# A list scheduler's model of DMA, a rule on PSUM banks, and a new table of tie offsets

## The chip, the cores and the metric

The kernel runs on one core of one Trainium2 chip. The metric is the device time of one execution in microseconds (us), lower is better. The time before is the median of three runs.

## What is computed

One layer of a streaming encoder for a prompt of 1024 frames and a sample of 32 frames with 512 frames of past, model width 1024. Half of the mixer is band attention (8 heads of 64, called A), half is stick-breaking attention (8 heads of 64, called B). All of it is in float32.

```python
u = rmsnorm(h, g_pre) @ w_in                     # q k v gate of A, q k v gate of B
# A: each frame reads its own 64-frame chunk and the 8 chunks before it
s = einsum(q, k) * scale + bias_table[:, rel];   w = softmax(where(ok, s, -1e30))
# B: strictly causal
z = einsum(q, k) * scale
log_beta = log_sigmoid(z);  log_1m = where(causal, log_sigmoid(-z), 0)
after = cumsum(log_1m, reverse) - log_1m
w = where(causal, exp(log_beta + after), 0)
o = einsum(w, v)
# end of the layer
y = concat([oa * silu(ga), ob * silu(gb)]) @ w_out
h = h + rmsnorm(y, g_post)
h = h + sigmoid(h @ w_ple_gate) * (p @ w_ple)
```

The new keys and values of both groups are outputs too.

## The kernel before

The 1056 rows (1024 of the prompt and 32 of the sample) are worked on as three chunks of 352. Every product in float32 is made of three products of rounded parts: high by high, high input by low weight, low input by high weight. Names with an h at the end (wTh, wh_kA, hnh) are high parts, with an l (wTl, wl_kA, hnl) low parts.

The work is cut into stages. The stage "first" loads x, normalises it, turns it on TensorE (ptx), makes the product of p with w_ple (ple) and the first projections (mm_kA, mm_qA, mm_vA). Stages 0 to 7 are the eight pairs of heads A0 B0 A1 B1 A2 B2 A3 B3; in each, the attention of the pair's two heads is woven with the projections of the next pair, and in the last stages with the gate projections (mm_gA, mm_gB; a chunk is 24 matmuls). The sample's heads come in between (names with an s: sA0, sB1). The stage "last" makes the output product and the gate product of the end, each cut Strassen-like into sets of seven products (o0P to o3P, then g0P to g3P).

A tile of attention is 128 queries against up to 1024 keys. Its name has the pair, the head and the tile: B31_4 is tile 4 of the second head of pair B3. TensorE makes the scores into a bank of PSUM called S, as a product with the keys' high part (kd) and one with their low part (kl). ScalarE, VectorE and GpSimd make the weights of them. The weights must then be turned. For most tiles TensorE does that (ptw). For tiles 5, 6, 7 of A and 4, 5, 6 of B, VectorE turns blocks of 32 x 32, one DMA writes the tile to a scratch in DRAM (swap), four DMAs read it back as the low tile wTl, ScalarE casts the high part out of it (wTh), and GpSimd or VectorE subtracts. Then sets of matmuls multiply with the values (PVA, PVB); a set takes several tiles. For keys, GpSimd makes the low part klB on one half of the partitions, and a DMA copies it to the other half (klB<-klB). Gate chunks go from PSUM through ScalarE (sg, three buffers in turn; sggA, sggB in the trace) and GpSimd, where they are multiplied with the attention's output (oggA, oggB, read back from the scratch o_dr), to the scratch og_dr, and from there as uo, lo, whole left inputs, into the output product. PSUM's eight banks are shared out as mm 2, S 3, T 2, PV 1; in the stage "last" the product sets and ple take turns at them too. The weights of the output product come as woB (the block whose two sums and casts give oB) and woT.

All DMAs go over one queue that SP fills. The order on every engine is set as follows. A recorder takes down every operation without issuing it (class Recorder). Then order(), line 478, runs a list scheduler: each engine has a heap of operations whose inputs are there at the engine's free time, and takes the one with the smallest key. The key is a class and the number at which it was recorded, plus an offset in AHEAD_OF by engine, first letters of the written tile's name, and stage. cost() gives each operation a duration. A DMA is modelled as an issue of 550 ns, 1500 ns more to its start (DMA_NS), one line for all transfers at 320 bytes a nanosecond, and 2000 ns to its completion (DMA_MARGIN). emit() (line 548) issues in this order; its line 558 is the line of all instructions in the trace. In the built program each engine runs its instructions in that order and waits on semaphores. A DMA also waits, on SP, for one of eight semaphores of the transfers eight places ahead.

Of the kernel before, what the change touches and what calls it, by code (L numbers as in the profile page):

```python
# [10 lines left out]
AF = mybir.ActivationFunctionType  # L11
# [15 lines left out]
NT = 9  # L27
STAGES = ("first", 0, 1, 2, 3, 4, 5, 6, 7, "last")
AHEAD_OF = {
# [4 lines left out]
    ("ACT", "hnh"): (26, 0, 0, 0, 0, 0, 0, 0, 0, 0),  # L34
# [4 lines left out]
    ("ACT", "pleo"): (-50, 0, 0, 0, 0, 0, 0, 0, 0, 0),  # L39
    ("ACT", "sg"): (0, 0, 0, 0, 0, 0, 0, 0, 0, 67),  # L40
    ("ACT", "stk"): (0, 0, 0, 0, -177, -400, 75, 0, 0, 0),
    ("ACT", "stq"): (0, 122, -152, -75, 154, 366, 0, 0, 0, 0),
    ("ACT", "stv"): (0, 0, 19, 0, 0, -79, 0, 25, 0, 0),
    ("ACT", "vt"): (234, 0, 0, 0, 0, 0, 0, 0, 0, 0),
    ("ACT", "wTh"): (0, 12, -62, 30, 74, -241, 0, 102, 0, 0),
    ("ACT", "wh"): (0, 0, 236, -23, 0, 0, 0, 0, 203, -9),
    ("ACT", "whS"): (0, 0, 0, 0, 0, 0, 0, 0, 0, 37),
    ("ACT", "x"): (0, 0, 0, 0, 0, 0, 0, 0, 0, -7),
    ("ACT", "yb"): (0, 0, 0, 0, 0, 0, 0, 0, 0, 427),
    ("DVE", "Kcs"): (0, 0, 0, 0, 402, 0, 0, 0, 102, 0),  # L50
# [5 lines left out]
    ("DVE", "diags"): (0, 0, 0, 400, 0, 0, 0, 0, 0, 0),  # L56
# [4 lines left out]
    ("DVE", "ogg"): (0, 0, 0, 0, 0, 0, 0, 0, 200, 0),  # L61
    ("DVE", "om"): (0, -187, -50, -41, -135, 385, -331, 253, -174, 0),
    ("DVE", "rb"): (265, 0, 0, 0, 0, 0, 0, 0, 0, 0),
    ("DVE", "sgg"): (0, 0, 0, 0, 0, 0, 0, 0, -180, 0),
# [4 lines left out]
    ("DVE", "wTl"): (0, -75, 64, 0, -385, 0, 0, 0, 0, 0),  # L69
# [8 lines left out]
    ("POOL", "ksS"): (0, 0, 0, 0, 0, 0, 0, 70, 0, 0),  # L78
    ("POOL", "om"): (0, 0, -289, 0, 0, 0, -89, 0, 0, 0),
    ("POOL", "ug"): (0, 0, 0, 0, 0, 0, 0, 0, 0, -100),  # L80
    ("POOL", "wTl"): (0, 493, 327, 0, 0, 0, 0, 0, 0, 0),
# [24 lines left out]
}  # L106


# [152 lines left out]


class Op:
    __slots__ = ("eng", "what", "args", "kw", "key", "busy", "late", "ready", "left", "after", "at", "size", "shared", "table", "kind")


LAND = {"PE": 165, "ACT": 0, "DVE": 0, "POOL": 0, "SP": 0, "CTL": 0}
SEM = 60
MARGIN = 400
ISSUE = 550  # L270
TABLE = 1280
DMA_NS, DMA_RATE, DMA_MARGIN = 1500, 320.0, 2000
DVE_SET, POOL_SET = 137, 110


# [78 lines left out]
class Recorder:  # L354
# [37 lines left out]
    def node(self, eng, what, args, kw, after):  # L392
        o = Op()
        o.eng, o.what, o.args, o.kw, o.after = eng, what, args, kw, after
        o.key = (self.cls if eng == "PE" else self.low, len(self.ops), len(self.ops))
        o.shared, o.table, o.kind = False, None, None
        self.ops.append(o)
        return o

    def add(self, eng, what, args, kw):  # L400
        writes, reads = [], []
# [7 lines left out]
        o = self.node(eng, what, args, kw, set())  # L409
# [20 lines left out]
        if writes:  # L430
            name = str(writes[0].buf.name)
            kind = (eng, name[:next((i for i, x in enumerate(name) if x.isdigit() or x in "AB_"), len(name))])
            o.kind = kind + (self.stage,)
            o.key = (o.key[0], o.key[1] + (AHEAD_OF[kind][STAGES.index(self.stage)] if kind in AHEAD_OF else 0), o.key[2])
        o.busy, o.late = self.cost(eng, method, args, kw, writes, reads)
        o.shared = eng == "POOL"
        if eng == "DVE":
# [4 lines left out]
    def cost(eng, method, args, kw, writes, reads):  # L442
# [20 lines left out]
        if eng == "POOL":  # L463
# [4 lines left out]
            if method == "tensor_scalar":  # L468
                return 255 + 0.86 * n, 0
            return 100 + 0.82 * n, 0  # L470
        size, run = 4, 0
        for v in (out, args[1]):
            if isinstance(v, View) and v.buf.pool is not None:
                size, run = 4 * v.shape[0] * v.free(), 4 * v.shape[-1]
        return ISSUE, max(size / DMA_RATE, size / run * (8.5 + 0.0365 * run) / 16)


    def order(self):
# [13 lines left out]
        for o in self.ops:  # L492
            if not o.left:
                heapq.heappush(soon[o.eng], (0.0, o.key, id(o), o))
        out, port, line, table = [], 0.0, 0.0, AF.Exp
        while len(out) < len(self.ops):
            best = None
            for e in names:
# [9 lines left out]
            while soon[e] and soon[e][0][0] <= t:  # L508
                _, key, n, o = heapq.heappop(soon[e])
                heapq.heappush(now[e], (key, n, o))  # L510
            o = heapq.heappop(now[e])[2]
            if o.shared and e == "DVE" and port > t + DVE_SET:
                held = [x for x in now[e] if not x[2].shared]
                if held:
                    heapq.heappush(now[e], (o.key, id(o), o))
                    pick = min(held)
                    now[e].remove(pick)
                    heapq.heapify(now[e])
                    o = pick[2]
            o.at = t  # L520
            if e == "CTL":
                done = t = o.ready
            elif e == "SP":
                free[e] = t + o.busy
                line = max(line, t + o.busy + DMA_NS) + o.late
                done = line + DMA_MARGIN
            else:
                if e == "ACT" and o.table not in (None, table):
                    t, table = t + TABLE, o.table
                if o.shared:  # L530
                    t = max(t, port - (DVE_SET if e == "DVE" else POOL_SET))
                    port = t + o.busy
                free[e] = t + o.busy
                done = t + o.busy + o.late
            out.append(o)
            for u in users[id(o)]:
                if u.eng == e and e != "SP":
                    r = t if e == "CTL" else free[e]
# [1514 lines left out]
```

## Time and profile before

| | |
|---|---|
| median of three runs | 804.09 us (803.0 to 805.33) |
| profiled execution | 804.02 us |
| its span, first to last instruction | 802.2 us |
| mean granted clock of TensorE | 0.995 |
| instructions | 14505, of them 4502 matmuls |
| DMA | 182.28 MB in 212960 packets, mean 227 GB/s |
| HBM | 109.79 MB read, 63.10 MB written |

The trace shows engines as PE (TensorE's matmuls), PEld (its weight loads, which overlap), DVE (VectorE), ACT (ScalarE), POOL (GpSimd) and SP (its queue's issues as SPq). Tile names stand without their numbers: klB is any head's. A row of the timeline has start, duration, engine, operation, the tile written and the tiles read, and in brackets the idle time before it with what ended it. A row of the chain has start, duration and what took it.

### The profile page before, as it was taken

Reading aid. Unit: us, or ns where it says so; the run is one execution under the profiler, and the core shown is the slowest. Engines: PE = TensorE matmul, PEld = TensorE weight load, DVE = VectorE, ACT = ScalarE, POOL = GpSimd, SP = SyncE. Lnnn points to the kernel's source line nnn. Section 1 sums busy time; section 2 is a strip of 40 time slices with the busy share of each in tenths; the row PEclk is TensorE's granted clock in tenths of the full one; section 3 lists DMA queues with packets and bytes.
Section 4 is the critical chain, followed back from the end, with each engine's and each line's share of the span. In section 5 each row is a group of like instructions: output and inputs, shape, how many; then the busy total and the mean of one; then the engine's idle time right before and its main releaser. Section 6 shows DMA issues by size and latency. Waiting matters only on the chain.

```text
span 802.2 us, 14505 instructions
## 1 busy us (share of the span) xinstructions
PE 769.0 (96%) x4502; PEld 705.2 (88%) x4502; DVE 560.6 (70%) x989; ACT 524.1 (65%) x1122; POOL 506.6 (63%) x545
## 2 busy tenths in 40 slices
PE   8999989999999999899999999889999899999997
PEld 6999979999889999889999998889897687888786
DVE  6727547786567678566695668769644788889965
ACT  6645856886777668776686585355425887776551
POOL 6532867994676557668895476568641439779533
PEclk9999999999999999999999999999999999999999
DMA  8738887878888558788968888889989976759753
GB/s 295 235 104 222 227 240 229 229 211 240 212 234 240 132 169 262 201 253 257 244 178 251 227 213 227 235 202 258 266 246 267 331 217 205 269 175 348 246 161 132
DMA packets 212960, 182.28 MB, mean 227 GB/s; under 512 B 69058, under 2 KB 175850, under 8 KB 212883
## 3 DMA queue, kind: packets, MB, share of 16 engines
q1 hardware_dynamic: 212882, 181.36, 78.5%
q8 instruction: 36, 0.59, 0.3%
q14 instruction: 42, 0.34, 0.1%
HBM read 109.79 MB, written 63.10 MB: 216 GB/s over the span
## 4 chain that ended last, share of the span: by engine, by line
PE 48%; DMA 20%; SPq 8%; DVE 7%; POOL 6%; ACT 6%; issue 4%; ACTq 0%; POOLq 0%; DVEq 0%
SPq L558 8%; PE mm_kA L558 4%; PE PVA L558 3%; PE mm_qA L558 3%; PE o0P L558 3%; DVE om L558 3%; PE o1P L558 2%; PE mm_kB L558 2%; PE g1P L558 2%; PE o3P L558 2%; PE g2P L558 2%; PE g0P L558 2%; PE o2P L558 2%; PE mm_vB L558 2%; PE g3P L558 2%
## 5 line engine op out<-in xcount | busy, mean ns | idle before, releaser
L558 DVE TENSOR_TENSOR_SCAN om<-om,SB 128x384 f32<-128x384 f32 (+5 forms) x96 | 91.6, 966 | 34.0 <-ACT be L558 11.4
L558 POOL TENSOR_TENSOR be<-be,om 128x1024 f32<-128x1024 f32 (+8 forms) x66 | 83.2, 1269 | 36.9 <-ACT be L558 13.2
L558 POOL TENSOR_TENSOR wTl<-wTl,wTh 128x640 fp32r<-128x640 f32 (+2 forms) x42 | 73.0, 1745 | 27.2 <-ACT wTh L558 23.3
L558 ACT ACTIVATE om<-SB 128x384 f32<-128x384 f32 (+5 forms) x96 | 45.0, 493 | 20.9 <-DVE SB L558 14.7
L558 ACT ACTIVATE be<-SB 128x384 f32<-128x384 f32 (+5 forms) x96 | 46.0, 497 | 11.9 <-DVE om L558 6.5
L558 ACT CAST wTh<-wTl 128x640 fp32r<-128x640 f32 (+2 forms) x48 | 37.2, 780 | 25.0 <-DMA wTl<-swapB 13.4
L558 ACT ACTIVATE be<-be,statA 128x640 f32<-128x640 f32 (+2 forms) x64 | 44.3, 695 | 7.6 <-DVE statA L558 7.4
L558 DVE STREAM_TRANSPOSE om<-be 128x640 f32<-128x640 f32 (+2 forms) x48 | 43.3, 903 | 4.7 <-POOL be L558 1.9
L558 DVE TENSOR_TENSOR wTl<-ptwA,wTh 128x512 fp32r<-128x512 f32 (+3 forms) x48 | 22.9, 483 | 22.6 <-ACT wTh L558 14.4
L558 POOL TENSOR_TENSOR oB<-oB,oB 128x256 f32<-128x256 f32 x32 | 23.6, 759 | 23.7 <-DMA oB<-in_w_out_dram 20.2
L558 PE MATMUL SB<-klB,LB 128*128 128x384 f32 (+5 forms) x96 | 32.4, 351 | 3.1 <-DMA klB<-klB 3.1
L558 PE MATMUL SB<-kdB,LB 128*128 128x384 f32 (+5 forms) x96 | 33.0, 351 | 1.6 <-DVE om L558 1.0
L558 DVE CUSTOM_DVE_ANT_0 be<-SA,biasA 128x320 f32<-128x320 f32 (+2 forms) x64 | 29.7, 477 | 6.0 <-POOL biasA L558 3.7
L558 DVE TENSOR_TENSOR SB<-SB,maskb 128x128 f32<-128x128 f32 x64 | 17.4, 290 | 19.3 <-PE SB L558 18.9
L558 PE MATMUL SA<-kdA,LA 128*128 128x320 f32 (+2 forms) x96 | 30.2, 320 | 0.3 <-DVE statA L558 0.2
L558 PE MATMUL SA<-klA,LA 128*128 128x320 f32 (+2 forms) x96 | 29.9, 313 | 0.0
L558 PE MATMUL PVB<-wTh,v2B 128*128 128x256 f32 (+1 forms) x144 | 22.4, 290 | 5.2 <-ACT wTh L558 5.2
L558 DVE TENSOR_TENSOR wTl<-ptwB,wTh 128x512 fp32r<-128x512 f32 (+3 forms) x48 | 25.5, 542 | 2.2 <-ACT wTh L558 2.2
L558 PEld LDWEIGHTS PVB<-wTh,v2B 128*128 128x128 f32 x144 | 20.6, 189 | 7.3 <-ACT wTh L558 6.7
L558 POOL TENSOR_TENSOR klA<-stkA,kdA 64x1024 fp32r<-64x1024 f32 (+2 forms) x9 | 19.4, 2151 | 11.8 <-ACT kdA L558 11.5
L558 ACT CAST wTh<-ptwB 128x512 fp32r<-128x512 f32 (+3 forms) x48 | 22.5, 485 | 6.5 <-PE ptwB L558 6.1
L558 POOL TENSOR_TENSOR sggB<-sggB,oggB 128x352 f32<-128x352 f32 x12 | 12.5, 1043 | 21.1 <-DMA og_dr<-sggB 8.2
(699 smaller groups left out, 2659.4 us busy)
## 6 DMA issues: line engine op xcount, KB each, us to landing
swapA<-om SPq DMA_DIRECT2D x24, 320.0 KB, 3.2
wTl<-swapA SPq DMA_DIRECT2D x96, 80.0 KB, 3.1
oggA<-o_dr SPq DMA_DIRECT2D x24, 176.0 KB, 4.4
oggB<-o_dr SPq DMA_DIRECT2D x24, 176.0 KB, 4.0
oB<-in_w_out_dram SPq DMA_DIRECT2D x16, 256.0 KB, 4.6
sum_dro<-oB SPq DMA_DIRECT2D x16, 256.0 KB, 3.1
o_dr<-otA SPq DMA_DIRECT2D x32, 128.0 KB, 3.1
o_dr<-otB SPq DMA_DIRECT2D x32, 128.0 KB, 3.0
```

Source lines behind the costliest of these rows:

```text
L558: getattr(getattr(tc.nc, o.what[0]), o.what[1])(*args, **kw)
```

## The change

The instructions are of the same kinds; their order changes on every engine. There are three edits.

First, the model of a DMA. A transfer starts 1700 ns after its issue, takes a share of 240 ns and then its bytes at 270 bytes a nanosecond between two places in SBUF, at 435 into SBUF and at 510 out of it (or by its short runs, now over 27 where it was over 16), and completes 1400 ns later. SP can issue only if fewer than eight transfers are under way.

Second, an operation that touches a PSUM buffer is put back until every other engine that uses the buffer is done with it by the model.

Third, the table AHEAD_OF is replaced as a whole: 76 rows before, 86 now. A row is a tuple with one offset for each stage.

```diff
-    ("SP", "wr"): (0, 0, 0, -288, -521, 0, 0, -254, 15, 0),
+    ("SP", "wr"): (0, 0, 0, -129, -452, 0, 0, -265, 35, 0),
...
-DMA_NS, DMA_RATE, DMA_MARGIN = 1500, 320.0, 2000
+DMA_NS, DMA_EACH, DMA_LANE, DMA_MARGIN = 1700, 240, 100, 1400
...
+        if eng != "SP":
+            o.banks = [b for b in dict.fromkeys(v.buf for v in reads + writes) if b.psum]
...
-        size, run = 4, 0
-        for v in (out, args[1]):
-            if isinstance(v, View) and v.buf.pool is not None:
+        size, run = 4, 4
+        inside = [isinstance(v, View) and v.buf.pool is not None for v in (out, args[1])]
+        for v, sbuf in zip((out, args[1]), inside):
+            if sbuf:
                 size, run = 4 * v.shape[0] * v.free(), 4 * v.shape[-1]
-        return ISSUE, max(size / DMA_RATE, size / run * (8.5 + 0.0365 * run) / 16)
+        rate = 270.0 if all(inside) else 435.0 if inside[0] else 510.0
+        return ISSUE, DMA_EACH + max(size / rate, size / run * (8.5 + 0.0365 * run) / 27)
...
+            clear = max([done for b in o.banks for x, done in banks.get(b, {}).items() if x != e], default=0.0)
+            if clear > t + 1e-6:
+                heapq.heappush(soon[e], (clear, o.key, id(o), o))
+                continue
...
             elif e == "SP":
-                free[e] = t + o.busy
                 line = max(line, t + o.busy + DMA_NS) + o.late
                 done = line + DMA_MARGIN
+                lanes = lanes[1:] + [line + DMA_LANE]
+                free[e] = max(t + o.busy, lanes[0])
...
             out.append(o)
+            for b in o.banks:
+                banks.setdefault(b, {})[e] = done + SEM
```

The line of emit() that issues is 579 after the change. Three places of the order follow. A row has the line, the operation, the tile written and the tiles read with their numbers, and the shape.

SP's queue at the start of head B00: kdB00 and klB00 are the copies of its keys' parts to the other half of the partitions, sum_dro a store of the weight sums for the output product, wr_qA1 a weight load, kdB01 the next head's keys. Before:

```order
L558 DMA kdB00_1071<-kdB00_1071 64x1024
L558 DMA sum_dro_85<-oB110_1068 128x512
L558 DMA wr_qA1_0_1212<-in_w_in_dram 128x4x128
L558 DMA wr_qA1_1_1235<-in_w_in_dram 128x4x128
L558 DMA one_dr0_71<-sumA00_233 16x32
L558 DMA kdB01_1238<-kdB01_1238 64x1024
L558 DMA klB00_1076<-klB00_1076 64x1024
```

and after:

```order
L579 DMA kdB00_1061<-kdB00_1061 64x1024
L579 DMA swapA01_7_116<-om_193 128x640
L579 DMA wr_qA1_0_1242<-in_w_in_dram 128x4x128
L579 DMA klB00_1064<-klB00_1064 64x1024
L579 DMA one_dr0_71<-sumA00_233 16x32
L579 DMA wr_qA1_1_1261<-in_w_in_dram 128x4x128
L579 DMA kdB01_1268<-kdB01_1268 64x1024
```

klB00 moved ahead of the second weight load, one_dr0 and kdB01; the store sum_dro of oB110 is no longer between. On TensorE, before, the scores of B00 with kd stand ahead of a projection chunk's end (mm_vB0_0) and of three tiles' turns (ptwA01_1 to _3):

```order
L558 MATMUL SB00_7_0_1315<-kdB00_1071,LB00_1077 128x512
L558 MATMUL ptwA01_1_0_1450<-ident_174,be_207 128x128
L558 MATMUL SB00_6_0_1259<-klB00_1076,LB00_1077 128x448
L558 MATMUL SB00_6_1_1276<-klB00_1076,LB00_1077 128x448
L558 MATMUL SB00_7_0_1315<-klB00_1076,LB00_1077 128x512
L558 MATMUL ptwA01_1_0_1450<-ident_174,be_207 128x128
L558 MATMUL mm_vB0_0_1340<-hnl0_171,wh_vB0_1_1150 128x352 x3
```

After, the chunk and the turns come first, and the scores with kd and kl follow each other:

```order
L579 MATMUL ptwA01_3_0_1431<-ident_174,be_207 128x128 x4
L579 MATMUL mm_vB0_0_1341<-hnh0_168,wh_vB0_1_1176 128x352 x3
L579 MATMUL mm_vB0_0_1341<-hnh0_168,wl_vB0_0_1127 128x352 x4
L579 MATMUL mm_vB0_0_1341<-hnh0_168,wl_vB0_1_1152 128x352 x4
L579 MATMUL mm_vB0_0_1341<-hnl0_171,wh_vB0_0_1168 128x352 x4
L579 MATMUL mm_vB0_0_1341<-hnl0_171,wh_vB0_1_1176 128x352 x4
L579 MATMUL SB00_6_0_1287<-kdB00_1061,LB00_1065 128x448
L579 MATMUL SB00_6_0_1287<-klB00_1064,LB00_1065 128x448
```

The three matmuls of the chunk and eight turns moved ahead of the first score that needs kl. In the gate stage, SP's queue at head B31 before (og_dr are stores of gates, oggB reloads for them):

```order
L558 DMA swapB31_5_164<-om_193 128x768
L558 DMA wr_gB3_0_7167<-in_w_in_dram 128x4x128
L558 DMA pp1_6342<-in_p_prompt_dram 32x32x32
L558 DMA og_dr_75<-sggA3_1_7036 128x352
L558 DMA oggB0_1_7192<-o_dr4_67 64x2x352 x2
L558 DMA wTl_184<-swapB31_6_163 32x4x224 x4
L558 DMA swapB31_4_165<-om_193 128x640
L558 DMA og_dr_75<-sggA3_2_7107 128x352
L558 DMA wTl_184<-swapB31_5_164 32x4x192 x4
```

After:

```order
L579 DMA swapB31_5_164<-om_193 128x768
L579 DMA swapB31_4_165<-om_193 128x640
L579 DMA wTl_184<-swapB31_6_163 32x4x224 x4
L579 DMA wr_gB3_0_7181<-in_w_in_dram 128x4x128
L579 DMA wr_gB3_1_7200<-in_w_in_dram 128x4x128
L579 DMA og_dr_75<-sggA3_1_7052 128x352
L579 DMA oggB0_1_7237<-o_dr4_67 64x2x352
L579 DMA wTl_184<-swapB31_5_164 32x4x192 x4
L579 DMA wTl_184<-swapB31_4_165 32x4x160 x4
L579 DMA og_dr_75<-sggA3_2_7124 128x352
```

The write of tile 4 moved right behind that of tile 5, and its reads ahead of the store of A3's last gate chunk. Ahead of the output product, SP's queue before:

```order
L558 DMA woB11_2_7757<-in_w_out_dram 128x512 x2
L558 DMA og_dr_75<-sggB3_1_7714 128x352
L558 DMA pp2_7787<-in_p_sample_dram 32x256
L558 DMA lo0_7797<-og_dr_75 128x4x128
L558 DMA lo1_7802<-og_dr_75 128x4x128
L558 DMA woT3_2_7809<-sum_dro_85 128x512 x2
L558 DMA ple_dr_90<-ple4_0_7564 128x512
L558 DMA og_dr_75<-sggB3_2_7748 128x352
L558 DMA uo0_7326<-og_dr_75 128x4x128
L558 DMA lo0_7797<-og_dr_75 128x4x128
L558 DMA woB11_3_7851<-in_w_out_dram 128x512 x2
```

After:

```order
L579 DMA og_dr_75<-sggB3_0_7687 128x352
L579 DMA og_dr_75<-sggB3_1_7748 128x352
L579 DMA lo0_7798<-og_dr_75 128x4x128
L579 DMA lo1_7803<-og_dr_75 128x4x128
L579 DMA uo1_7812<-og_dr_75 128x4x128
L579 DMA woB11_3_7829<-in_w_out_dram 128x512 x2
L579 DMA ple_dr_90<-ple4_0_7595 128x512
L579 DMA pp2_7844<-in_p_sample_dram 32x256
L579 DMA ple_dr_90<-ple4_1_7596 128x512
L579 DMA og_dr_75<-sggB3_2_7777 128x352
```

The load of woB11_3 moved ahead of the store of the last gate chunk (sggB3_2).

More of the change, by code (lines that the diff above doesn't have):

```diff
@@ L29 @@
 AHEAD_OF = {
[4 rows of a table removed]
-    ("ACT", "hnh"): (26, 0, 0, 0, 0, 0, 0, 0, 0, 0),
[4 rows of a table removed]
[L39 to L50, printed above, removed]
[5 rows of a table removed]
-    ("DVE", "diags"): (0, 0, 0, 400, 0, 0, 0, 0, 0, 0),
[4 rows of a table removed]
[L61 to L64, printed above, removed]
[4 rows of a table removed]
@@ L69 @@
-    ("DVE", "wTl"): (0, -75, 64, 0, -385, 0, 0, 0, 0, 0),
[8 rows of a table removed]
[L78 to L81, printed above, removed]
[21 rows of a table removed]
+    ("ACT", ""): (0, 0, 0, 0, 0, 0, 0, 0, 0, -27),
+    ("ACT", "Kh"): (0, 0, 0, 0, 0, 0, 0, 83, 0, 0),
+    ("ACT", "L"): (0, 0, -37, -70, 427, 0, 140, 0, 0, 0),
+    ("ACT", "Qfs"): (0, 0, 0, 0, 100, 0, 0, 0, 0, 0),
@@ new lines @@
+    ("ACT", "Qhs"): (0, 0, 0, 0, 0, 0, 0, 0, 420, 0),
[9 rows of a table added]
+    ("ACT", "stk"): (0, 0, 100, 0, -99, 0, 79, 0, 0, 0),
+    ("ACT", "stq"): (0, 232, -315, 0, 400, 440, 400, 0, 0, 0),
+    ("ACT", "stv"): (0, 0, 0, 0, 0, 0, 0, 22, 0, 0),
+    ("ACT", "v"): (0, 0, 0, 0, 0, 0, 0, 149, 0, 0),
+    ("ACT", "vt"): (464, 0, 0, 0, 0, 370, 0, 0, 0, 0),
+    ("ACT", "wTh"): (0, 0, -111, 9, 428, 0, 74, 49, 75, 0),
[3 rows of a table added]
+    ("DVE", ""): (0, 0, 0, 0, 0, 0, 0, 0, 0, 100),
[6 rows of a table added]
+    ("DVE", "diags"): (0, 0, 0, 0, 0, 0, 0, 0, -432, 0),
@@ new lines @@
+    ("DVE", "g"): (0, 0, 0, 0, 0, 0, 0, 0, 0, 41),
+    ("DVE", "gT"): (0, 0, 0, 0, 0, 0, 0, 0, 0, -106),
+    ("DVE", "hnl"): (54, 0, 0, 0, 0, 0, 0, 0, 0, 0),
+    ("DVE", "lg"): (0, 0, 0, 0, 0, 0, 0, 0, 0, 559),
+    ("DVE", "newl"): (0, 0, 0, 0, 0, 0, 0, 0, 116, 0),
+    ("DVE", "oT"): (0, 0, 0, 0, 0, 0, 0, 0, 0, 492),
+    ("DVE", "ogg"): (0, 0, 0, 0, 0, 0, 0, 0, 162, 0),
+    ("DVE", "oj"): (0, 0, 0, 0, 0, 0, 0, 0, 0, 100),
+    ("DVE", "om"): (0, 0, 0, -51, -17, 722, -178, 133, 0, 0),
+    ("DVE", "pleo"): (-250, 0, 0, 0, 0, 0, 0, 0, 0, 0),
[5 rows of a table added]
@@ L103 @@
+    ("DVE", "wTl"): (0, 0, 0, -446, -456, 0, -159, -201, 106, 0),
[8 rows of a table added]
+    ("POOL", "Qfs"): (0, 0, 0, 0, 0, 0, 0, 0, 75, 0),
[3 rows of a table added]
+    ("POOL", "qsS"): (0, 0, 67, 0, 0, 0, -400, 0, 0, 0),
+    ("POOL", "ug"): (0, 0, 0, 0, 0, 0, 0, 0, 0, -216),
+    ("POOL", "w"): (0, 0, 0, 0, 0, 0, 0, 0, 378, 0),
+    ("POOL", "wTl"): (0, 0, 0, 0, 0, 0, 111, 0, 0, 0),
[20 rows of a table added]
     ("SP", "wpr"): (-10, 0, 0, 0, 0, 0, 0, 0, 0, 0),
[2 rows of a table removed]
[2 rows of a table added]
 }
@@ L263 @@
 class Op:
-    __slots__ = ("eng", "what", "args", "kw", "key", "busy", "late", "ready", "left", "after", "at", "size", "shared", "table", "kind")
+    __slots__ = ("eng", "what", "args", "kw", "key", "busy", "late", "ready", "left", "after", "at", "size", "shared", "table", "kind", "banks")
 LAND = {"PE": 165, "ACT": 0, "DVE": 0, "POOL": 0, "SP": 0, "CTL": 0}
@@ L395, in node @@
         o.key = (self.cls if eng == "PE" else self.low, len(self.ops), len(self.ops))
-        o.shared, o.table, o.kind = False, None, None
+        o.shared, o.table, o.kind, o.banks = False, None, None, ()
         self.ops.append(o)
@@ L494, in order @@
                 heapq.heappush(soon[o.eng], (0.0, o.key, id(o), o))
-        out, port, line, table = [], 0.0, 0.0, AF.Exp
+        out, port, line, table, lanes, banks = [], 0.0, 0.0, AF.Exp, [0.0] * 8, {}
         while len(out) < len(self.ops):
```

106 rows, old and new, of the table AHEAD_OF are left out of this document.

## The prediction

> **What bounds the kernel now.** I read the page first: busy time, then the chain that ended last.
>
> ```profile
> PE 769.0 (96%) x4502; PEld 705.2 (88%) x4502; DVE 560.6 (70%) x989; ACT 524.1 (65%) x1122; POOL 506.6 (63%) x545
> ...
> PE 48%; DMA 20%; SPq 8%; DVE 7%; POOL 6%; ACT 6%; issue 4%; ACTq 0%; POOLq 0%; DVEq 0%
> ```
>
> TensorE (PE) is the bound: 769.0 us busy of a span of 802.2, by 4502 matmuls that the change leaves as they are. The chain names DMA for 20%, yet most of that lies beside matmuls. So a new order can move only what TensorE stands idle, and what it loses to its clock. Next I read TensorE's waits (columns: what waited and for what; us in total, times, longest).
>
> ```profile
> PE PVB L558 <- ACT wTh L558: 5.2, 4, 1.8
> PE o0P L558 <- ACT ple L558: 3.2, 1, 3.2
> PE PVA L558 <- ACT wTh L558: 3.1, 3, 2.0
> PE SB L558 <- DMA klB<-klB: 3.1, 1, 3.1
> PE ptx L558 <- DVE be L558: 1.9, 2, 1.3
> ...
> PE ptx L558 <- DVE hnl L558: 0.2, 1, 0.2
> ```
>
> The view has 20 rows, the first and the last of them shown; they add up to 27.3 us in 29 waits. That is all an order can win here, but for the clock. For the clock I read busy time in stretches (stretch, length, busy time and count of PE, PEld, DVE, ACT and POOL, then the granted clock, the DMA share, GB/s).
>
> ```profile
> 107.71:111.13 3.42, 3.42 (x11) 3.13 (x12) 0.30 (x1) 1.29 (x3) 1.42 (x2) 0.50 0.88 256
> 111.20:114.60 3.40, 3.40 (x24) 3.37 (x23) 1.01 (x1) 2.75 (x7) 1.47 (x1) 1.00 0.85 236
> 626.50:629.96 3.46, 3.46 (x9) 2.66 (x9) 2.86 (x5) 3.31 (x8) 3.30 (x4) 0.51 1.09 372
> 630.00:633.40 3.40, 3.40 (x16) 2.77 (x15) 1.42 (x1) 1.55 (x4) 0.87 (x1) 1.00 1.10 349
> 337.00:340.40 3.40, 3.40 (x21) 3.23 (x22) 0.19 (x1) 3.32 (x6) 3.40 (x3) 1.00 0.57 157
> 660.00:680.00 20.00, 20.00 (x89) 14.60 (x88) 16.03 (x26) 15.34 (x33) 19.23 (x26) 1.00 0.59 192
> ```
>
> After each of the two idle times of over 3 us, the one ahead of 107.71 and the one ahead of 625.07, TensorE works for 3.4 us at half clock: 11 matmuls where the next stretch has 24, and 9 where it has 16. Half of 3.4 is 1.7 us lost, twice. The idle 2.0 us ahead of 337 cost no clock. [...] From 640 us on TensorE is full (the row at 660), and order can win nothing there. After its last matmul,
>
> ```profile
> 796.89 0.29 PE L558 MATMUL g3P3b<-gB,wlS4g 128*128 128x256 f32 x1
> ```
>
> come some 5 us of the other engines' last work, in an order that the change keeps.
>
> **The change, term by term.** Three waits change their cause; I take each from what stands ahead of its last transfer.
>
> *The first scores of head B00.* Rows of the chain, of GpSimd (POOL) and of SP's issues:
>
> ```profile
> 91.69 2.83 POOL L558 TENSOR_TENSOR oB<-oB,oB 128x256 f32<-128x256 f32 x4
> 94.48 2.37 POOL L558 TENSOR_TENSOR klB<-stkB,kdB 64x1024 fp32r<-64x1024 f32 x1
> 97.78 0.56 SPq L558 DMA_DIRECT2D sum_dro<-oB  x1
> 98.39 2.08 SPq L558 DMA_DIRECT2D wr_qA<-in_w_in_dram  x2
> 100.58 0.43 SPq L558 DMA_DIRECT2D one_dr<-sumA  x1
> 101.13 0.47 SPq L558 DMA_DIRECT2D kdB<-kdB  x1
> 101.69 5.98 DMA klB<-klB
> 107.71 1.54 PE L558 MATMUL SB<-klB,LB 128*128 128x448 f32 x3 [3.09 <-DMA klB<-klB]
> ...
> 111.25 0.49 PE L558 MATMUL ptwA<-ident,be 128*128 128x128 f32 x3
> 112.23 1.46 PE L558 MATMUL mm_vB<-hnh,wl_vB 128*128 128x352 f32 x8
> ```
>
> The copy of klB to the other 64 partitions is issued at 101.69, behind five transfers that nothing on TensorE waits for yet, though POOL had it at 96.85. After, one store of the sums (98.39 - 97.78 = 0.6 us), one of two weight loads (half of 100.58 - 98.39: 1.1), one_dr (0.55) and the copy of the next head's kdB (0.55) stand behind it: 2.8 us earlier, so issued at 98.9 and landed, with the same 5.98, at 104.9. POOL makes klB after one of the four sums (2.83 us) instead of after all of them, so it is not what klB waits for. TensorE got there at 107.71 - 3.09 = 104.62. It gets there later now: eight more turns of weights (0.08 us each, from 0.24 us between the starts at 111.25 and the next) and three more projection matmuls (0.16 each, 1.46 by 8 less overlap) stand ahead, together 1.1 us. So 105.7 against 104.9: the wait goes with 0.8 us to spare, and with it the clock loss: 3.1 + 1.7 = **4.8 us**. Cover: if the copy lands over 0.8 us later, that part comes back. [...]
>
> *The first output product, o0P.* Rows of ScalarE (ACT) and SP:
>
> ```profile
> 607.70 1.86 SPq L558 DMA_DIRECT2D woB<-in_w_out_dram  x2
> 613.31 0.48 SPq L558 DMA_DIRECT2D og_dr<-sggB  x1
> 616.10 0.83 SPq L558 DMA_DIRECT2D woB<-in_w_out_dram  x2
> ...
> 621.42 1.33 ACT L558 CAST oB<-woB 128x512 fp32r<-128x512 f32 x2 [1.57 <-DMA woB<-in_w_out_dram]
> 622.88 0.62 ACT L558 CAST whA11o<-uo 128x512 fp32r<-128x512 f32 x1
> 624.44 0.58 ACT L558 COPY ple<-ple 128x512 f32<-128x512 f32 x1
> 625.07 4.26 PE L558 MATMUL o0P<-oB,A11o 128*128 128x512 f32 x12 [3.17 <-ACT ple L558]
> ```
>
> o0P needs a PSUM bank that ACT empties at 624.44 (ple7_1), and ACT was held until 621.42 by the last block of w_out (woB11_3), issued at 616.10. After, that load stands ahead of the store of the last gate (613.31) and of the reloads behind it. Those took from 613.31 to 616.10, 2.8 us, and some 0.5 us more for a store that also moves behind: about 3 us earlier. ACT's own wait of 1.57 us goes, and one of three casts between (0.6) goes ahead; that makes 2.2 us, and leaves 1 us of the 3.17. With a gap of 1 us the half clock goes too: 2.2 + 1.7 = **3.9 us**.
>
> *Weights of head B31.* A "turned" tile goes through DVE, a DMA out and four DMAs in, then an ACT cast:
>
> ```profile
> 557.09 0.83 DVE L558 STREAM_TRANSPOSE om<-be 128x640 f32<-128x640 f32 x1
> 562.15 0.34 SPq L558 DMA_DIRECT2D swapB<-om  x1
> 562.59 0.38 SPq L558 DMA_DIRECT2D og_dr<-sggA  x1
> 570.02 1.37 SPq L558 DMA_DIRECT2D wTl<-swapB  x3
> ...
> 571.44 4.26 DMA wTl<-swapB
> 575.85 0.73 ACT wTh L558
> 576.63 1.74 PE PVB L558 x12
> ```
>
> DVE had the tile at 557.9, SP wrote it out at 562.15 and read it back from 570.02 on; this is the 1.8 us wait in the first row of TensorE's waits. After, the write stands ten rows earlier, right behind that of the tile before, and the reads ten rows earlier too. SP needs 570.02 - 562.15 = 7.9 us for the 13 rows between, 0.6 each, so the reads could come up to 6 us earlier; the write itself can gain at most 562.15 - 557.9 = 4.2. The product, however, also stands nearer behind its scores. I take 1.5 of 1.8: **1.5 us**.
>
> *What is given back.* Without the three, 27.3 - 8.1 = 19.2 us of waits are left in 26, 0.74 each; I take their sum as it is, since their places are shuffled. Four places get tighter by the order (the weights of B01's second set, B30, B31 and the sample's B1 stand nearer behind their scores): 4 x 0.74 = **3.0 us** back. At the start, the loads of two more x tiles stand ahead of the first key weights; bounds are +1 us (the second of them is one 0.95 us issue at most) and -1, half of the 1.9 us that ptx waits for; I take 0. The rule on PSUM banks and the new DMA costs act only through the order and cost no instruction.
>
> Sum: the profiled execution took 804.02 us (span 802.2 and 1.8 around it), and the median of the runs is 804.09, so one base serves both. 804.02 - 4.8 - 3.9 - 1.5 + 3.0 = **796.8 us**.
>
> **The rivals.**
>
> *Slower: gate stores behind the reads.* At 545 to 600 us each gate chunk goes through ACT and POOL and is stored; its buffer (three of them) comes free only when the store has landed. Already now:
>
> ```profile
> 562.46 0.47 ACT L558 ACTIVATE sggB<-mm_gB 128x352 f32<-128x352 f32 x1 [3.88 <-DMA og_dr<-sggA]
> ```
>
> The store of A3's last chunk stood right behind B31's write (562.59); now eight reads come ahead of it. If each of the twelve chunks of gate B holds its PSUM bank 1 us longer than TensorE can bear (two banks, 24 matmuls a chunk), that is 12 us, and one wait past 3 us costs 1.7 more: 796.8 - 3.0 + 13.7 = 807.5. It ends slower once over 12.6 us (10.2 won and 2.4) come back. For it: the 3.88 us. Against it: in before that wait did not reach TensorE's first rows.
>
> *No change.* What removed waits uncover arrives as late: DMA time varies more (4.26 to 5.98 us in the rows above) than the rows moved. The klB copy lands 1 us later than I take, the bank of o0P is late by another load, and both stay past 3 us; then about 803 us. This is also the case in which the change does not do what it says: the order moves, the times do not.
>
> *Larger gain.* If the planner's times are now near the chip's, the 26 small waits halve (-9.6) and nothing comes back: 804.0 - 10.2 - 9.6 = 784. Against it: rows of casts behind DMA round trips keep their length.
>
> **How the numbers follow.** Forecast, all three waits mostly gone: 0.48, on its own 792 to 801. Larger gain: 0.15 (784 to 792). No change: 0.18, of which a third ends past 0.3% on the faster side. Slower: 0.19. About 0.3% (2.4 us) is what a measurement of this kernel can tell. Faster 0.48 + 0.15 + 0.05 = 0.68; same 0.13; slower 0.19. The range leaves out half of the larger gain and over half of the slower case: 788 to 806.
>
> **What would show it.** Right: TensorE's waits no longer list klB, the stretch behind it has clock 1.00, o0P waits 1 us or less and the stretch behind it has clock 1.00, the PVB waits lose their 1.8, and the sum of waits is near 20 us. Wrong: either stretch at half clock still, mm_gA or mm_gB waiting on sgg by several us, or a sum of waits over 27.

## The result, and the profile after

| | before | after |
|---|---|---|
| median of four runs | 803.68 us (803.0 to 805.33) | 792.11 us (789.85 to 793.41) |
| profiled execution | 804.02 us | 793.41 us |
| span | 802.2 us | 791.6 us |
| granted clock, mean | 0.995 | 0.992 |

The ratio is 0.985, with a 95% interval of 0.9822 to 0.9878: 1.5% faster. The profiled execution is the slowest of the four after the change, and 10.6 us under that of before.

The page of the changed kernel, busy time and chain:

```profile
PE 765.9 (97%) x4502; PEld 707.6 (89%) x4502; DVE 563.0 (71%) x989; ACT 524.3 (66%) x1122; POOL 503.8 (64%) x545
...
PE 68%; DMA 14%; SPq 6%; DVE 5%; ACT 3%; issue 3%; POOL 1%; DVEq 0%; ACTq 0%
```

TensorE's share of the chain rose from 48% to 68%, and its busy time fell by 3.1 us with the same 4502 matmuls. Its waits:

```profile
PE PVB L579 <- ACT wTh L579: 4.5, 3, 2.8
PE SB L579 <- DVE om L579: 3.9, 4, 1.9
PE mm_gB L579 <- DVE sggB L579: 2.4, 2, 1.8
PE PVA L579 <- ACT wTh L579: 2.1, 2, 1.3
PE ptx L579 <- DVE be L579: 1.7, 1, 1.7
...
PE mm_vA L579 <- ACT wh_vA L579: 0.2, 1, 0.2
```

Two rows of before stand beside them:

```profile
PE SB L558 <- DVE om L558: 1.0, 2, 0.8
PE mm_gA L558 <- DVE sggA L558: 0.7, 1, 0.7
```

The rows for klB and for o0P are gone. The sum of the view fell from 27.3 to 20.2 us. SB behind VectorE's scan (om) grew from 1.0 to 3.9 us. The wait of mm_gB behind the gates (sggB) is new; in before only mm_gA stood behind its gates, for 0.7 us. PVB's row, the one that holds B31's weights, fell by less, from 5.2 to 4.5. A part of each wait stands in the busy time: the next of TensorE's matmuls with 352 columns follows after 0.16 us in a full row, but the last one before a wait is counted to its end, some 0.16 us more. Ahead of the waits of the view this makes 4.5 us in before and 3.6 after. Over all matmuls at full clock that are counted over 0.06 us longer than the median of their shape, the excess is 22.8 us in before and 19.0 after; most of it stands where the view has no wait, and the traces do not show what it comes from.

The head of B00, on SP and on TensorE:

```profile
95.62 1.15 SPq L579 DMA_DIRECT2D klB<-klB  x1
96.88 0.52 SPq L579 DMA_DIRECT2D one_dr<-sumA  x1
...
112.73 0.50 PE L579 MATMUL SB<-kdB,LB 128*128 128x512 f32 x1 [1.87 <-DVE om L579]
```

klB is issued 6 us earlier than before, and no score waits for it. Nine microseconds on, the second scores wait 1.87 us. Ahead of the output product, on ACT and TensorE:

```profile
611.91 0.62 ACT L579 CAST oB<-woB 128x512 fp32r<-128x512 f32 x1
612.44 0.58 ACT L579 COPY ple<-ple 128x512 f32<-128x512 f32 x1
612.92 0.62 ACT L579 CAST oB<-woB 128x512 fp32r<-128x512 f32 x1
...
615.67 2.70 PE L579 MATMUL o0P<-oB,A11o 128*128 128x512 f32 x11
```

ACT no longer waits for woB there, and o0P follows ple at once. In the gate stage:

```profile
554.53 0.46 ACT L579 ACTIVATE sggB<-mm_gB 128x352 f32<-128x352 f32 x1 [3.72 <-DMA og_dr<-sggA]
555.61 1.56 PE L579 MATMUL mm_gB<-hnh,wh_gB 128*128 128x352 f32 x8 [1.77 <-DVE sggB L579]
560.52 1.17 PE L579 MATMUL PVB<-wTh,v2B 128*128 128x256 f32 x8 [0.94 <-ACT wTh L579]
```

B31's weights cost 0.94 us where they cost 1.80, and the gates now cost 1.77: the store of a gate holds the buffer, ACT waits for it (3.72 us), VectorE's product of the gate waits for ACT, and TensorE for the bank that this product reads. Last, the clock, in stretches that begin where the clock changes:

```profile
110.11:113.52 3.41, 1.54 (x9) 1.17 (x8) 2.25 (x3) 2.90 (x6) 1.88 (x2) 1.00 0.84 244
113.52:116.93 3.41, 3.41 (x13) 3.41 (x12) 2.26 (x3) 2.07 (x5) 2.92 (x2) 0.50 0.99 211
372.94:376.35 3.41, 1.76 (x13) 1.44 (x12) 1.09 (x1) 3.41 (x7) 1.84 (x2) 1.00 1.06 343
376.35:379.76 3.41, 3.41 (x14) 3.27 (x14) 2.19 (x4) 2.21 (x6) 3.41 (x5) 0.50 1.05 303
516.29:519.71 3.42, 1.14 (x8) 1.00 (x8) 1.68 (x4) 2.71 (x7) 2.49 (x2) 1.00 0.46 133
519.71:523.12 3.41, 3.41 (x14) 3.41 (x15) 1.92 (x4) 0.78 (x2) 2.20 (x2) 0.50 0.78 209
553.84:557.25 3.41, 1.64 (x11) 1.64 (x11) 0.96 (x2) 0.46 (x1) 1.18 (x2) 1.00 1.01 325
557.25:560.67 3.42, 2.48 (x18) 2.12 (x17) 0.59 (x2) 0.94 (x1) 2.64 (x5) 1.00 1.08 278
```

There are three half-clock stretches of 3.41 us now, one more than before; they cost 5.1 us instead of 3.4. None follows a wait of 3 us. They follow stretches in which TensorE was busy for 0.45, 0.52 and 0.33 of the time; after one of 0.48, at 553.84, the clock stayed.

Where the time went is best read at equal work. I gave each matmul the median time, of those of before that write a tile of the same name, from its start to the next one's, and took, at the start of the matmul that stands behind so much work, how far the trace is behind that sum. The columns are growth within a stretch, in us; work is counted from TensorE's first matmul.

| stretch of work, us | before | after | won |
|---|---|---|---|
| 0 to 75 (start) | 5.1 | 4.2 | 0.9 |
| 75 to 125 (head of B00) | 5.1 | 3.2 | 1.9 |
| 125 to 525 | 25.5 | 24.6 | 0.9 |
| 525 to 575 (gates, B31) | 4.8 | 3.0 | 1.8 |
| 575 to the end (output product) | 4.9 | -0.2 | 5.1 |

The last column adds up to the 10.5 us by which TensorE ends earlier, but for rounding.

The table is of one execution each. The experiments below left more traces of both orders, and at places that their edits leave alone the same sums can be taken from them. At the start the old order costs 5.1, 6.5 and 6.6 us, the new one 3.6 to 4.3 in seven traces. In the stretch of the output product the old order costs 4.9 and 3.2 us, the new one -0.5 to 0.1 in six. So these two gains repeat. From 125 to 525 the old order costs 24.4 to 27.0 us, the new one 24.3 to 25.1: the 0.9 us is less than executions differ by. In the stretch of gates and B31 it is 4.8, 2.0 and 4.5 us against 2.1 to 3.0: a gain there is not shown.

### The profile page after: what moved, and what is told of

Read it like the earlier page. It is cut to its first block, busy times and chain, and to the rows that moved or that the text cites. A ratio compares the mean times of both kernels' runs of the same rounds, so it can differ in the third digit from the quotient of the medians.

```text
span 791.6 us, 14518 instructions
## 1 busy us (share of the span) xinstructions
PE 765.9 (97%) x4502; PEld 707.6 (89%) x4502; DVE 563.0 (71%) x989; ACT 524.3 (66%) x1122; POOL 503.8 (64%) x545
## 4 chain that ended last, share of the span: by engine, by line
PE 68%; DMA 14%; SPq 6%; DVE 5%; ACT 3%; issue 3%; POOL 1%; DVEq 0%; ACTq 0%
SPq L579 6%; PE mm_vA L579 6%; PE mm_qA L579 5%; PE mm_kA L579 4%; PE mm_kB L579 4%; PE mm_qB L579 3%; PE PVB L579 3%; PE SA L579 3%; PE PVA L579 3%; PE mm_vB L579 3%; PE SB L579 3%; PE g1P L579 2%; PE o1P L579 2%; PE o3P L579 2%; PE g2P L579 2%
## 5 line engine op out<-in xcount | busy, mean ns | idle before, releaser
L579 POOL TENSOR_TENSOR wTl<-wTl,wTh 128x640 fp32r<-128x640 f32 (+2 forms) x42 | 71.3, 1703 | 27.7 <-ACT wTh L579 21.7
L579 ACT ACTIVATE om<-SB 128x512 f32<-128x512 f32 (+5 forms) x96 | 45.2, 499 | 14.7 <-DVE SB L579 9.2
L579 ACT CAST wTh<-wTl 128x640 fp32r<-128x640 f32 (+2 forms) x48 | 37.6, 783 | 18.9 <-DMA wTl<-swapB 13.7
L579 POOL TENSOR_TENSOR oB<-oB,oB 128x256 f32<-128x256 f32 x32 | 24.0, 770 | 25.5 <-DMA oB<-in_w_out_dram 20.6
L579 DVE TENSOR_TENSOR wTl<-ptwA,wTh 128x512 fp32r<-128x512 f32 (+3 forms) x48 | 22.8, 481 | 18.5 <-ACT wTh L579 13.4
L579 DVE CUSTOM_DVE_ANT_0 be<-SA,biasA 128x320 f32<-128x320 f32 (+2 forms) x64 | 29.8, 481 | 4.3 <-POOL biasA L579 1.3
L579 POOL TENSOR_TENSOR gB<-gB,gB 128x256 f32<-128x256 f32 x32 | 24.1, 771 | 7.5 <-DMA gB<-in_w_ple_gate_dram 4.2
L579 PE MATMUL PVB<-wTl,v2B 128*128 128x256 f32 (+1 forms) x144 | 27.0, 308 | 0.3 <-DVE wTl L579 0.2
L579 POOL TENSOR_TENSOR klB<-stkB,kdB 64x1024 fp32r<-64x1024 f32 x8 | 20.0, 2502 | 10.1 <-ACT kdB L579 9.9
```

The source lines that it names most:

```text
L579: getattr(getattr(tc.nc, o.what[0]), o.what[1])(*args, **kw)
```

## The experiments

Two kinds were made: whole parts of the change alone, and single steps moved. For the second a helper between order() and emit() moves named steps of the finished order. In the diffs a step is its engine, the tile written and, where needed, the tile read; "up to" puts it ahead of another step or as near as its inputs allow, "down to" right behind it. All other steps keep their order.

**Rules and table apart.** Four kernels: the new rules with the old table, the old rules with the new table, and either set of rules with no offsets.

```diff
 # rules_only: after.py
-AHEAD_OF = { new table }
+AHEAD_OF = { old table }
 # table_only: before.py
-AHEAD_OF = { old table }
+AHEAD_OF = { new table }
 # before_no_offsets, after_no_offsets
-AHEAD_OF = { ... }
+AHEAD_OF = {}
```

> The new DMA model, the limit of eight and the rule on banks, with the old table of offsets. Theory A (the gain lies in a few waits that the offsets were fitted to remove, and offsets fit only the rules that they were found with): about the old time or worse, 800 to 820 us. Rival B (the truer model makes the better order whatever the offsets): 790 to 797 us.

> The old rules with the new table of offsets. Theory A (offsets fit only their own rules): 800 to 825 us. Rival C (the table alone carries the gain, the new rules hardly matter): 790 to 797 us.

> The old rules with an empty table of offsets: the list scheduler alone. Theory A: 815 to 840 us, since every place that offsets had mended shows. Rival B expects more here than with the new rules by at least 8 us.

> The new rules with an empty table of offsets. Theory A: within 5 us of the old rules without offsets, 812 to 840 us. Rival B (the model carries the gain): at least 8 us below the old rules without offsets.

| | no offsets | old table | new table |
|---|---|---|---|
| old rules | 851.73 | 804.02 | 838.38 |
| new rules | 823.93 | 820.35 | 792.11 |

Against the kernel before, the ratios are 1.0593 (1.0502 to 1.0684) for the old rules bare, 1.0247 (1.0131 to 1.0364) for the new rules bare, 1.0203 (1.0118 to 1.0287) for the new rules with the old table, and 1.0427 (1.0308 to 1.0546) for the old rules with the new table. The changed kernel's 792.11 us is from another series of runs, in which the kernel before took 803.68; every bare or crossed kernel has two runs. For the crossed pairs theory A is right in kind: a table found with one set of rules is worth 3.6 us with the other rules (less than two runs can tell), or 13. In size it missed. The new table with the old rules took 838.4 us where A gave 800 to 825, the old rules bare 851.7 where it gave 815 to 840, and the old table with the new rules 820.4, just over its 800 to 820. For the bare pair it falls: I had expected the two within 5 us, and the new rules are 27.8 us ahead (rival B: at least 8). So the new rules make a better order bare. The old table took 47.7 us off the old rules, the new table takes 31.8 us off the new. The 11.6 us of the change belong to rules and table together. The three new rules (the model of a DMA, the limit of eight, the banks) were not tried apart. Nor was a table fitted anew to the old rules, so it is not shown that the old rules could not have come as far with more fitting.

**kl_early**: the kernel before with the prediction's first term alone.

```diff
+    SP klB00      up to SP kdB00
```

> The kernel before with one DMA moved: the copy of klB00 right behind that of kdB00 on SP's queue, five places earlier. Theory P (the prediction's first term): the wait of 3.1 us goes and with it 1.7 us of half clock, so -4.8 us, 799 us, and the stretch behind has clock 1.00. Rival Q (the next wait takes its place): the scores then wait 1 to 2 us for a bank that VectorE's scan holds, the stretch stays at half clock, and the time falls by 1 to 2 us only. Rival R: other transfers put back by the move return all of it, 0 us.

The median is 803.11 us against 803.76, a ratio of 1.0009 (0.9974 to 1.0044): no gain that these runs can tell, and by the interval not the 4.8 us of theory P. Rows of SP, TensorE, ACT and VectorE:

```profile
98.96 0.58 SPq L601 DMA_DIRECT2D klB<-klB  x1
...
105.66 0.89 PE L601 MATMUL SB<-klB,LB 128*128 128x448 f32 x3
...
116.93 0.50 PE L601 MATMUL SB<-kdB,LB 128*128 128x512 f32 x1 [2.83 <-DVE om L601]
...
121.02 1.50 PE L601 MATMUL PVA<-wTh,v2A 128*128 128x512 f32 x8 [1.11 <-ACT wTh L601]
...
112.41 0.37 ACT L601 COPY otA<-PVA 128x256 f32<-128x256 f32 x1 [4.33 <-DMA o_dr<-otA]
112.68 0.55 ACT L601 ACTIVATE om<-SB 128x448 f32<-128x448 f32 x1
...
114.61 2.27 DVE L601 TENSOR_TENSOR_SCAN om<-om,SB 128x448 f32<-128x448 f32 x2 [7.95 <-ACT om L601]
```

klB is issued at 98.96, as the prediction worked out for the change (98.9), and its wait is gone. But the next scores now wait 2.83 us for the bank that VectorE's scan holds, and the weights behind them 1.11. This is rival Q, with a larger wait than it gave. At equal work the stretch from 75 to 125 costs 4.4 us against 5.1. Its clock stays whole here (at 118.21 us seven matmuls of mm_vB take 1.37 us, as eight take 1.46 ahead of the wait), which Q did not expect. The rows also show what VectorE is late for: ACT's copy of an output (otA) stands ahead of its second function of the scores (om) and waits 4.33 us until a store has freed its buffer, and the scan waits for om. In before ACT comes to this copy at 111.17 us, after the wait for klB, and does not wait for the store.

**ple_first**: the kernel before, with ACT's last steps ahead of o0P in another order.

```diff
+    ACT ple7_1    up to ACT whA11o1
+    ACT A11o0     up to ACT whA11o1
```

> The kernel before with ACT's last steps ahead of the output product in another order: the bank of ple7_1 emptied and A11o0 cast ahead of two casts of uo1. The wait of o0P should fall from 3.17 to about 2.1 us. Theory W (TensorE's clock is set by its busy share in fixed stretches of 3.41 us; under about half it halves): that stretch is then 0.7 busy, the clock stays, -1.0 - 1.7 = -2.7 us. Rival G (a wait of about 2 us is enough to halve the clock, as at 112.73 after the change): half clock stays, -1.0 us.

The median is 806.5 us, a ratio of 1.0057 (1.0021 to 1.0092): 0.6% slower. The wait was split, not shortened:

```profile
623.25 0.59 ACT L601 COPY ple<-ple 128x512 f32<-128x512 f32 x1 [1.77 <-DMA ple_dr<-ple]
...
624.41 0.74 PE L601 MATMUL o0P<-oB,A11o 128*128 128x512 f32 x2 [1.88 <-ACT A11o L601]
626.75 1.65 PE L601 MATMUL o0P<-oB,A11o 128*128 128x512 f32 x3 [1.60 <-DVE A11o L601]
```

The first wait is 1.88 us, near what both theories gave, though ACT now waits 1.77 us for a store before it can empty the bank of ple7_1; then the third matmul waits 1.60 us for A11o0's low part, which needs xA11o0's difference on VectorE and comes no earlier. Together 3.48 us against 3.17, and TensorE was busy for only 0.22 of the stretch ahead of 626.50; half clock stays (the three matmuls at 626.75 take 1.65 us, where the two at 624.41 took 0.74). The 0.3 us between these sums is not the 2.7 us by which the median is slower. Part of that may be that 3.17 us is one execution's wait: in kl_early, which leaves this place alone, o0P waited 1.80 us for the same bank. The run does not tell W from G, since its busy share is not the one that W supposed.

**wo_late**: the changed kernel with the load of the second term put back.

```diff
+    SP woB11_3    down to SP og_dr<-sggB3_2
```

> The changed kernel with the load of woB11_3 put back behind the store of the last gate chunk (sggB3_2) on SP, as before the change. Theory P (the prediction's second term: the 5 us that TensorE no longer loses ahead of the output product come from that load's place): ACT gets it some 2.8 us later, o0P waits 2 to 2.8 us again, with or without half clock: +2.2 to +4.5 us, 794.3 to 796.6. Rival S (the place of the load does not matter; the gain there came from the rest of the order): within 0.5 us of 792.1.

On ACT, TensorE and in TensorE's waits:

```profile
611.74 0.62 ACT L622 CAST oB<-woB 128x512 fp32r<-128x512 f32 x1 [2.99 <-DMA woB<-in_w_out_dram]
...
614.27 0.69 PE L622 MATMUL ple<-wph0False,php 128*64 128x512 f32 x1 [2.19 <-DVE php L622]
```

```profile
PE ple L622 <- DVE php L622: 2.2, 1, 2.2
```

ACT waits 2.99 us for the load again, and TensorE 2.19 us behind it, followed by 3.41 us at half clock. At equal work the stretch from 575 to the end costs 3.5 us instead of -0.2: 3.7 us, within theory P's 2.2 to 4.5. The wait falls one step ahead of o0P, on ple8's left input (php), because ACT makes that one behind the casts too. The whole time shows less of it: 792.71 us, ratio 0.9869 (0.9829 to 0.991), beside 0.985 (0.9822 to 0.9878), since the rest of this execution lost less than that of the change (29.8 against 32.1 us at 525 of work, by waits that the edit doesn't touch). So the load's place is shown at its place; the medians cannot tell.

**ot_late**: the changed kernel, the wait that took klB's place.

```diff
+    ACT otA00_0_1 and SP o_dr<-otA00_0_1   down to ACT omB00_7<-SB00_7_0
```

> The changed kernel with ACT's copy otA00_0_1, which waits 2.95 us for a store, behind the first six sigmoids of B00 instead of ahead of them; its store on SP moves with it. Theory Q (the wait of 1.87 us of the second scores of B00 for VectorE's scan comes from that copy holding up ACT): the wait goes and the half clock behind it too, -1.9 - 1.7 = -3.6 us, 788.5 us. Rival R: the scan is late for itself, or the late copy holds PVA, and the wait stays or comes back within 20 us: 0 to -1 us.

The median is 788.69 us, ratio 0.9809 (0.9766 to 0.9853). The stretch from 75 to 125 costs 0.5 us, and the wait of 1.87 is gone; one of 0.64 is left later:

```profile
117.24 0.45 PE L622 MATMUL SB<-kdB,LB 128*128 128x384 f32 x1 [0.64 <-DVE om L622]
```

That looks like theory Q's 3.6 us. But in the profiles of wth_early, reads_early, stk_early and wo_late, which leave this place as the change made it, the same wait is 1.42, 1.23, 1.23 and 0.57 us, without half clock, and the stretch costs 0.4 to 1.3 us. So the 3.2 us in the profile of the change were mostly that execution's chance; the copy's place is worth under 1 us. The intervals of the two ratios overlap. The mechanism of Q is borne out all the same. In the change the copy's row is:

```profile
106.43 0.37 ACT L579 COPY otA<-PVA 128x256 f32<-128x256 f32 x1 [2.95 <-DMA o_dr<-otA]
```

In those four profiles the copy waits 2.50, 2.31, 2.32 and 1.66 us for its store, and TensorE's wait is 1.08 or 1.09 us less than that in all five. So what varies is when ACT gets the buffer back from the store.

**wth_early and reads_early**: the changed kernel's longest wait, PVB at 518 us.

```diff
 # wth_early
+    ACT wThB30_1<-wTlB30_1 (the second)   up to ACT wh_gA3_0
 # reads_early, besides
+    SP wTlB30_1<-swapB30_4 x4             up to SP wr_gA3_0
```

> The changed kernel with ACT's cast wTh of B30's tile 4 ahead of two weight casts that wait 3.9 us for wr_gA3. Theory Q (the PVB wait of 2.8 us is that of ACT's queue, not of the tile's own transfers): the wait falls under 0.5 us, the half clock behind goes, -2.4 - 1.7 = -4.1 us, 788 us. Rival R: the tile's reads land as late as the weights, the cast holds up ACT, and the wait stays over 2 us: 0 us.

> The changed kernel with the four reads of B30's tile 4 ahead of the two weight loads wr_gA3 on SP, and its cast wTh ahead of the casts of those weights on ACT. Theory T (the 2.8 us of the PVB wait are the tile's own transfers, which stand behind two loads of over 8 us; moving the cast alone did nothing): the wait falls under 0.5 us and the half clock behind goes: -2.4 - 1.7 to -3.4 = -4.1 to -5.8 us, 786.3 to 788. Rival U (all transfers share one rate, and the loads that now come later hold up mm_gA3): a new wait on mm_gA of 1 to 2 us, -1 to -3 us.

The medians are 789.44 us (0.9826, 0.9778 to 0.9874) and 790.43 us (0.9856, 0.9823 to 0.989). With the cast moved, ACT just waits for the reads; wth_early's row:

```profile
516.11 0.72 ACT L622 CAST wTh<-wTl 128x640 fp32r<-128x640 f32 x1 [6.02 <-DMA wTl<-swapB]
```

TensorE's wait is 3.05 us there: rival R. With the reads ahead of the weight loads as well, the rows of reads_early's chain and TensorE are:

```profile
509.94 6.35 DMA wTl<-swapB
...
517.16 0.93 PE L622 MATMUL PVB<-wTh,v2B 128*128 128x256 f32 x6 [1.29 <-ACT wTh L622]
517.93 0.28 PE L622 MATMUL PVB<-wTl,v2B 128*128 128x128 f32 x1
519.71 1.44 PE L622 MATMUL PVB<-wTl,v2B 128*128 128x256 f32 x5 [1.51 <-DVE wTl L622]
```

The last read still takes 6.35 us to land, where the median of all reads of B's tiles of this size is 2.6 us in this trace, though it stands ahead of the loads on the queue. The wait falls to 1.29, a second of 1.51 comes behind it, half clock stays (four matmuls of mm_gA take 1.38 us at 520.95, where eight took 1.45 at 514.42). No wait of mm_gA comes, so rival U does not hold either. four_moves, which has the same edit, shows the like: reads of 5.7 to 6.5 us, waits of 0.43 and 1.54. Behind the loads these reads took 6.7 to 8.2 us in five traces. So by these figures their place on the queue is worth about 1 us of landing, and theory T falls: most of the time stays, with the two weight loads issued right behind the reads (510.48 us). Why was not separated.

**stk_early and four_moves**: a small wait, and all mends together.

```diff
 # stk_early
+    ACT stkA3<-mm_kA3_2   up to ACT wThB20_2<-wTlB20_2
 # four_moves: ot_late, reads_early and stk_early together
```

> The changed kernel with ACT's eviction of mm_kA3's last chunk (stkA) ahead of the cast wTh of B20's last set instead of five steps behind it; ACT stands idle there for 2.6 us. Theory W (clock by the busy share of a fixed stretch; here 0.52, and with the wait of 0.86 us gone about 0.77): the wait goes and the half clock at 376 us with it, -0.9 - 1.7 = -2.6 us, 789.5. Rival G (the clock falls for another reason, such as the two waits' places): half clock stays, -0.9 us.

> The changed kernel with the three mends together: the late copy otA00_0_1, the early reads and cast of B30's tile 4, the early stkA. If they add up: -3.4 (measured for the late copy) - 4.1 - 2.6 = -10 us, 782 us. Rival (each mend uncovers the next wait, as the early copy of klB00 did in the kernel before): -4 to -6 us, 786 to 788.

stk_early: 789.69 us, 0.9852 (0.9811 to 0.9893). The wait of 0.86 us is gone, one of 0.93 stands nearby (PVB, behind GpSimd), and the clock at that place stays whole, as W gave:

```profile
373.80:377.20 3.40, 3.40 (x25) 3.29 (x25) 1.99 (x6) 2.33 (x6) 3.40 (x3) 1.00 0.89 243
```

But in ot_late and wo_late, which leave this place alone, the clock stayed whole too, so the edit is not shown to be the cause. four_moves: 788.09 us (783.83 to 790.86), 0.9818 (0.9767 to 0.9869); its profiled execution has the shortest span of all, 782.0 us, with TensorE busy 98% of it:

```profile
PE 762.8 (98%) x4502; PEld 706.3 (90%) x4502; DVE 562.5 (72%) x989; ACT 523.7 (67%) x1122; POOL 504.3 (64%) x545
```

It is the best by its median, about 2 us more off the kernel before than the change takes (13.5 us beside 11.6 us, each against its own runs of before), less than either the sum (10) or the rival (4 to 6) gave; the intervals overlap, so it is not shown to beat the change.

## Why the prediction was right, and where it was not

The direction, two of the three places and the range were right: 792.1 us lies in 788 to 806. The forecast of 796.8 was 3.4 us over the profiled execution and 4.7 over the median. That it came so near is in part luck: in the profiled execution its first term is 2.9 us too large, and what it gave back, 3.0 us, did not come. By its steps:

- *Only idle time and clock can be won.* Right: of the 10.5 us by which TensorE ends earlier, 7.1 are waits. The rest, 3.1 us of busy time, I had not counted. 0.9 us of it is the matmuls ahead of waits, of which there are six fewer; the third half-clock stretch takes 1.7 back; the other 3.9 us are not traced to a cause.
- *First term, 4.8 us.* The mechanism held as far as klB goes: issue (6 us earlier, where I had 2.8), landing, no wait. The price was wrong. kl_early shows that the move alone brings nothing that can be told, because the next scores then wait for VectorE, VectorE for ACT and ACT for a store; I had asked what was late next only for klB itself. This is what the no-change rival supposed, at one place. In the profiled execution half clock came all the same, behind the second scores. With the rest of the order (the chunk and turns ahead of the scores among it) the profiled execution wins 1.9 us there, other executions with the same order at that place 3.8 to 4.7.
- *Second term, 3.9 us.* Right in mechanism and near in size: 5.1 us won, and wo_late brings back 3.7 of it by this one load. I had left a wait of 1 us for ACT, and there was none. Against kl_early's execution of the old order, where o0P waited 1.80 us, it is 3.4.
- *Third term, 1.5 us.* 1.8 us won in that stretch, though not as stated: B31's wait fell by 0.9 and not to nothing, and the slower rival's mechanism took 1.77 us in the same stretch, gates behind their stores. It came at two places (1.77 and 0.68 us) and stayed small, so the rival's sum of 13.7 us never arose. And the 1.8 us are not shown to be the change's: kl_early's execution of the old order cost 2.0 us there, less than the changed kernel's 3.0. What repeats is the exchange: B31's wait is 1.18 to 2.33 us in three traces of the old order and 0.40 to 0.94 in six of the new, and the wait for the gates 0.96 to 1.83 us in these six.
- *Given back, 3.0 us.* This is the step of the sum that failed. From 125 to 525 of work the change loses nothing that stands out of the spread of executions (it wins 0.9 us in the profiled one, in spite of two new half-clock stretches), and it wins 0.9 at the start, which I took as nothing. Of my four places B30 did get tighter (0.95 us before, 2.80 after), but I had counted no place that gets looser. Had I set it at nothing, the sum would have been 793.8.
- *Half clock needs an idle time of 3 us.* Wrong. A wait of 1.87 us was enough at 112.73, and two of 0.8 and 0.9 us at 374 and 376.
- *The change does what it says.* For the bare rules, taken as a whole, yes and more than I would have given: 27.8 us. In the kernel as it was, the old table had already made good most of that.

## What to carry to other kernels

Where one engine is busy 96% of the time, list its waits and price a new order by them; but before you book a removed wait as a gain, move that one step alone or name the buffer that the next instructions will need, on each engine of the chain, since the wait here only went to the next bank, by way of ACT's buffer. Offsets fitted to a scheduler's model are part of that model: fit them again after any change of it, and judge a model without them. Where a place varies by a microsecond from execution to execution, compare it in all the traces that leave it alone before you credit an edit with it.

## What the runs showed of the hardware

In each of fourteen traces the half-clock stretches begin at whole multiples of 3.413 us from one another, to within 0.1% of a stretch: 77.00 and 119.00 of them, for example, between those of the changed kernel at 113.52, 376.35 and 519.71. The busy share of the grid's stretch ahead goes with it (counted from 10 us on in all fourteen; a stretch ahead may itself be one at half clock):

| TensorE busy in the stretch | followed by half clock |
|---|---|
| under 0.4 | 34 of 34 |
| 0.4 to 0.5 | 20 of 21 |
| 0.5 to 0.6 | 7 of 25 |
| 0.6 to 0.8 | 9 of 118 |
| over 0.8 | 3 of 3009 |

Of the 19 stretches busy over half that half clock follows, 14 are at half clock themselves, where the same matmuls count as busy for about twice as long (in the prediction's rows 11 fill a stretch at half clock, and 24 the next one). Taken apart: of the stretches at full clock, half clock follows 48 of 49 with TensorE busy under half, 4 of 22 at 0.5 to 0.6, 1 of 110 at 0.6 to 0.8 and none of 2953 above. Of those at half clock, it goes on behind all 17 that are busy under 0.8, and behind 3 of 56 above.

So in these traces the length of a wait alone does not tell whether half clock follows: behind the 1.87 us of the change at 112.73 it did, behind 2.0 us of before at 337 it did not. The first lay in a stretch of which TensorE was busy for 0.45; the second is shared by two, and before's trace has them 0.57 and 0.84 busy:

```profile
333.00:336.41 3.41, 1.96 (x13) 1.67 (x11) 0.56 (x2) 1.94 (x6) 2.36 (x2) 1.00 0.81 253
336.41:339.83 3.42, 2.87 (x18) 2.74 (x19) 0.00 (x0) 3.37 (x6) 2.84 (x3) 1.00 0.69 205
```

A full stretch at half clock costs 1.7 us, half of 3.41. The grid lies elsewhere in each of the two executions: counted back by whole stretches from 107.72 us in before it begins 1.91 us into the span, from 113.52 us in after 0.88. What sets the clock was not separated beyond these counts.

The same place with the same order varies. In the kernel before, PVA waited 2.0 us at 337 with the clock whole; in kl_early and ple_first, which leave it alone, 3.23 and 3.09 us, with 6.83 and 3.41 us at half clock about them:

```profile
PE PVA L601 <- ACT wTh L601: 5.8, 4, 3.2
```

This row is of kl_early's waits. One such place can cost an execution some 3 us (in ple_first 1.1 us more of wait and half of 3.41), as much as most of the edits here.
